# A decoder block on one core: the first modulation row on TensorE, an affine on ScalarE, and lambda computed first

## Chip, core and metric

One NeuronCore of a Trainium2 chip runs the whole kernel. The metric is the device time of one execution in microseconds (us); the median of three runs stands for the kernel. TensorE multiplies matrices, VectorE and GpSimd work elementwise, ScalarE evaluates activations and copies, and SyncE's queue issues most of the DMAs.

## What is computed

The reference is a transformer block on 512 tokens of 1024 channels. What the change touches is the modulation at its start, and lambda, which is used in the differential attention:

```python
cond = jax.nn.silu(c)
mod = cond @ ada_w[l] + ada_b[l]                 # 1024 -> 6 * 1024
sh1, sc1, gt1, sh2, sc2, gt2 = jnp.split(mod[:, None, :], 6, axis=-1)
h = rmsnorm(x, norm1_w[l]) * (1.0 + sc1) + sh1
qa, ka, va, qm, km, vm, om, ip, fp, ga, gm = split_cols(h @ w_in[l], IN_SIZES)
...
lam = (jnp.exp(jnp.sum(lam_q1[l] * lam_k1[l]))
       - jnp.exp(jnp.sum(lam_q2[l] * lam_k2[l])) + lam_init)
y_a = diff_attention(qa, ka, va, lam, subln_w[l], lam_init)
```

After that come the mLSTM branch, the merge, an output projection, a second modulated norm and a PEER expert layer (128 keys, dense for three token tiles, gathered for one).

## The kernel before

The kernel holds 512 tokens as four tiles of 128 (NT) and 1024 channels as eight tiles of 128 (KD). It is written in a tile framework that plans at compile time: it simulates the program with its own costs, and writes out one fixed order of instructions for each engine and one for each DMA queue. Each queue then runs in that order, and an instruction whose operand is late holds everything behind it on its engine. The lines of the source are therefore not the order of execution: for example the memsets of L427 run in the first microseconds. DMAs from SyncE's queue are issued in the planned order too.

**The start stage** (pool `start`, L229 to L303) prepares `hT`, the normalised and modulated input with channels on partitions, and makes the first projections of it: the mLSTM gates (`psg`, called `gate` in the trace), the first head pair's q and the first head pair's k.

- `xt` (four loads of 512 KB) is squared on ScalarE (L265), scaled by the rms (L268), transposed on TensorE (32 transposes, L272), and copied to `xT` on ScalarE (L273).
- The modulation rows are made on VectorE. `ada_early(half)` loads, for shift (`accs[0]`) and scale (`accs[1]`), eight tiles of `ada_w` of 128x512 (256 KB), and `ada_step` (L215 to L219) adds `w * cond` to an accumulator: 8 steps for each of the four (half, row) pairs, 32 in all. Each accumulator still has 128 partitions; `ada_cols` (L221) sums these and turns four columns of 128 channels onto partitions by fp32 matmuls with a column of ones, which write `adac`; VectorE adds the bias (L225).
- Channels 0 to 511 are half 0, channels 512 to 1023 are half 1. For each half, L289 finishes the scale, ScalarE writes `hT_hi` (L291, rounded to fp32r), VectorE repeats the affine at full precision in place in `xT` (L292), and VectorE or, where k % 3 is 2, GpSimd writes `hT_lo = xT - hT_hi` (L293).
- Then the matmuls of this half: `mm3` makes each product out of three fp32r matmuls (hi*hi, hi*lo, lo*hi). Half 0 has 12 of the gate and 48 each of q and k, half 1 the same.
- The weights are split the same way: `load_w` takes raw pieces of 512 KB from two `raw` buffers; ScalarE casts `hi`; VectorE (L181) or GpSimd (L138) subtracts to make `lo`. For k the first piece's `lo` is GpSimd's and the second one's is VectorE's.

**Lambda** (L312 to L324) is computed behind this stage: two products and two sums on one partition of VectorE, an Exp on ScalarE (with its table load), two small VectorE operations, a scaling of `subw`, a matmul that spreads the value to 128 partitions (`psl`), and a copy to `neglam`.

**What follows.** The mix stage handles four head pairs with attention, mLSTM and gates, up to about 640 us. In it `ada_late` (L372) streams the other modulation rows, in 64 loads with two buffers, between the weight pieces on SyncE's queue. The expert layer follows to the end, with TensorE busy 96% of it.

Of the kernel before, what the change touches and what calls it, by code (L numbers as in the profile page):

```python
# [10 lines left out]
F32 = mybir.dt.float32  # L11
# [5 lines left out]
AF = mybir.ActivationFunctionType  # L17
OP = mybir.AluOpType
AX = mybir.AxisListType
PSUM = bass.MemoryType.PSUM  # L20

P = 128
S = 512
D = 1024
KD = D // P
# [5 lines left out]
LAM_INIT = 0.8 - 0.6 * math.exp(-0.3 * 0)  # L31
# [30 lines left out]
def block_kernel(ctx: ExitStack, tc: tile.TileContext, a, out, dbg=None):  # L62
    nc = tc.nc
    dbg = dbg or {}
    V, A, G, T = nc.vector, nc.scalar, nc.gpsimd, nc.tensor
# [13 lines left out]
    def ftile(shape, dt=F32, name=None):  # L79
        return fconst.tile(shape, dt, name=name)  # L80
# [12 lines left out]
    ones = ftile([P, P], F32, "ones")  # L93
# [10 lines left out]
    def load_const(name, shape, src):  # L104
        t = ftile(shape, F32, name)
        nc.sync.dma_start(t, src)
        return t

    cT = load_const("cT", [P, KD], a["cT"])
    cond = ftile([P, KD], F32, "cond")  # L110
# [5 lines left out]
    def rstd(dst, ssq, n, width):  # L116

        V.tensor_scalar(dst, ssq, 1.0 / n, EPS, op0=OP.mult, op1=OP.add)
        G.tensor_tensor(dst, dst, nhalf[:, 0:width], op=OP.pow)
# [15 lines left out]
    def split(hi, lo, src, eng=V):  # L135

        A.copy(hi, src)  # L137
        eng.tensor_tensor(lo, src, hi.bitcast(F32), op=OP.subtract)  # L138
# [5 lines left out]
    def acc_tile(name):  # L144
        return ps_acc.tile([P, 512], F32, tag="acc", name=name)

    def tr_tile(name):
        return ps_tr.tile([P, 512], F32, tag="tr", name=name)


    sh1 = ftile([P, KD], F32, "sh1")
    sc1 = ftile([P, KD], F32, "sc1")
    neglam = ftile([P, 1], F32, "neglam")
# [32 lines left out]
    def mm3(ps, l_hi, l_lo, r_hi, r_lo, start, stop):  # L186
        T.matmul(ps, l_hi, r_hi, start=start, stop=False)  # L187
        T.matmul(ps, l_hi, r_lo, start=False, stop=False)
        T.matmul(ps, l_lo, r_hi, start=False, stop=stop)
# [25 lines left out]
    def ada_step(acc, w, k):  # L215
        if k == 0:
            V.tensor_scalar(acc, w, cond[:, 0:1], None, op0=OP.mult)
        else:
            V.scalar_tensor_tensor(acc, w, cond[:, k:k + 1], acc, op0=OP.mult, op1=OP.add)  # L219

    def ada_cols(acc, n, b0, dst):  # L221
        ps = tr_tile(f"adac_{b0}")
        for k in range(n):
            T.matmul(ps[:, k:k + 1], acc[:, k * P:(k + 1) * P], ones[:, 0:1], start=True, stop=True)
        V.tensor_tensor(dst, ps[:, 0:n], adabT[:, b0:b0 + n], op=OP.add)  # L225


    psg = ps_sc.tile([P, 2, S], F32, tag="sc", name="gate")[:, 0]
    with tc.tile_pool(name="start", bufs=1, side="right") as sp:  # L229
        xts = []  # L230
        for t in range(NT):
            xt = sp.tile([P, D], F32, name=f"xt{t}")
            nc.sync.dma_start(xt, a["x"][t * P:(t + 1) * P, :])
            xts.append(xt)
        adabT = load_const("adabT", [P, 48], a["adabT"])
        n1w = load_const("n1w", [P, KD], a["n1T"])
        accs = [sp.tile([P, D], F32, name=f"ada_acc{i}") for i in range(2)]

        def ada_early(half):
            hs = slice(half * 512, (half + 1) * 512)  # L240
            for i in range(2):
                for k in range(KD):
                    w = sp.tile([P, 512], F32, tag="ada_w", bufs=24, name="ada_w")
                    nc.sync.dma_start(w, a["ada_w"][k * P:(k + 1) * P, i * D + half * 512:i * D + (half + 1) * 512])
                    ada_step(accs[i][:, hs], w, k)
        ada_early(0)
        graw = sp.tile([P, KD, 16], F32, name="graw")
        nc.sync.dma_start(graw, a["w_gate"])
        w_q, w_k = [load_w(w_in, PIECES.index((o,)), n) for o, n in ((O_QA, "q0"), (O_KA, "k0"))]
        ada_early(1)  # L250
        n2w = load_const("n2w", [P, KD], a["n2T"])
        ib = load_const("ib", [8, 1], a["ib"])
        fb = load_const("fb", [8, 1], a["fb"])
        cos_t = load_const("cos_t", [P, NT, 8], a["cos"])
        sin_t = load_const("sin_t", [P, NT, 8], a["sin"])
        lamv = load_const("lamv", [1, 4, 64], a["lamv"])
        convw = load_const("convw", [P, KD, 4], a["convw"])
        convb = load_const("convb", [P, KD], a["convb"])
        subw = load_const("subw", [P, P], a["subln_w"].partition_broadcast(P))
        ssq1 = sp.tile([P, NT], F32, name="ssq1")  # L260
        rs1 = sp.tile([P, NT], F32, name="rs1")
        junk = sp.tile([P, D], BF16, name="junk")
        xT = sp.tile([P, KD, S], F32, name="xT")
        for t in range(NT):
            A.activation(junk, xts[t], AF.Square, accum_out=ssq1[:, t:t + 1])  # L265
        rstd(rs1, ssq1, D, NT)
        for t in range(NT):
            A.activation(xts[t], xts[t], AF.Copy, scale=rs1[:, t:t + 1])  # L268
        for k in range(KD):
            ps = tr_tile("xTp")  # L270
            for t in range(NT):
                T.transpose(ps[:, t * P:(t + 1) * P], xts[t][:, k * P:(k + 1) * P], ident)  # L272
            A.copy(xT[:, k], ps)  # L273


        g_hi, g_lo = [sp.tile([P, KD, P], F32R, name=n) for n in ("g_hi", "g_lo")]
        G.memset(g_hi.bitcast(F32), 0.0)
        G.memset(g_lo.bitcast(F32), 0.0)
        for j in range(2):
            split(g_hi[:, :, j * 32:j * 32 + 8], g_lo[:, :, j * 32:j * 32 + 8], graw[:, :, j * 8:j * 8 + 8])  # L280

        ps_q = [acc_tile(f"q0_{t2}").rearrange("p (t c) -> p t c", t=2) for t2 in range(2)]
        ps_k = ps_sc.tile([P, 2, S], F32, tag="sc", name="k0").rearrange("p b (t c) -> p b t c", t=2)
        ps_k = [ps_k[:, 0], ps_k[:, 1]]
        for half in range(2):
            ks, ks4 = range(4 * half, 4 * half + 4), slice(4 * half, 4 * half + 4)
            ada_cols(accs[0][:, half * 512:], 4, 4 * half, sh1[:, ks4])
            ada_cols(accs[1][:, half * 512:], 4, 8 + 4 * half, sc1[:, ks4])
            V.scalar_tensor_tensor(sc1[:, ks4], sc1[:, ks4], 1.0, n1w[:, ks4], op0=OP.add, op1=OP.mult)  # L289
            for k in ks:  # L290
                A.activation(hT_hi[:, k], xT[:, k], AF.Identity, scale=sc1[:, k:k + 1], bias=sh1[:, k:k + 1])  # L291
                V.tensor_scalar(xT[:, k], xT[:, k], sc1[:, k:k + 1], sh1[:, k:k + 1], op0=OP.mult, op1=OP.add)  # L292
                (G if k % 3 == 2 else V).tensor_tensor(hT_lo[:, k], xT[:, k], hT_hi[:, k].bitcast(F32),  # L293
                                                       op=OP.subtract)
            for k in ks:
                mm3(psg, g_hi[:, k], g_lo[:, k], hT_hi[:, k], hT_lo[:, k], k == 0, k == KD - 1)
            for pss, (whi, wlo) in ((ps_q, w_q), (ps_k, w_k)):
                for t in range(NT):
                    ts_ = slice(t * P, (t + 1) * P)
                    for k in ks:  # L300

                        mm3(pss[t // 2][:, t % 2], hT_hi[:, k, ts_], hT_lo[:, k, ts_], whi[k], wlo[k],
                            k == 0 and t % 2 == 0, k == KD - 1 and t % 2 == 1)  # L303
# [3 lines left out]
    mrg = mrgp.tile([P, NT, D], F32, name="mrg")  # L307
    lx = ExitStack()
    lp = lx.enter_context(tc.tile_pool(name="mix", bufs=1))


    lq = ftile([1, 2, 64], F32, "lp")  # L312
    V.tensor_tensor(lq, lamv[:, 0::2, :], lamv[:, 1::2, :], op=OP.mult)
    ls = ftile([1, 2], F32, "ls")
    V.tensor_reduce(ls, lq, axis=AX.X, op=OP.add)
    le = ftile([1, 2], F32, "le")
    A.activation(le, ls, AF.Exp)
    nl = ftile([1, 1], F32, "nl")
    V.tensor_tensor(nl, le[:, 1:2], le[:, 0:1], op=OP.subtract)
    V.tensor_scalar(nl, nl, LAM_INIT, None, op0=OP.subtract)  # L320
    V.tensor_scalar(subw, subw, 1.0 - LAM_INIT, None, op0=OP.mult)
    psl = tr_tile("psl")
    T.matmul(psl[:, 0:1], ones[0:1, :], nl, start=True, stop=True)
    V.tensor_copy(neglam, psl[:, 0:1])  # L324

    Gr, lf = [lp.tile([P, NT, 256], F32, tag=t_, bufs=1, name=n).rearrange("p t c -> p (t c)")[0:8, 0:S]
              for n, t_ in (("Gr", "g0"), ("lf", "g1"))]
# [341 lines left out]
    for hp in range(4):  # L669
# [26 lines left out]
        for t in range(NT):  # L696
            for u in range(2):
                us = slice(u * P, (u + 1) * P)
                V.scalar_tensor_tensor(ga[:, t, us], y_a[:, t, us], rs[:, 0, t, u:u + 1], ga[:, t, us],  # L699
                                       op0=OP.mult, op1=OP.mult)  # L700
                V.scalar_tensor_tensor(gm[:, t, us], y_m[:, t, us], rs[:, 1, t, u:u + 1], gm[:, t, us],
                                       op0=OP.mult, op1=OP.mult)
# [181 lines left out]
    for k4 in range(2):  # L884
# [3 lines left out]
        ps = tr_tile("hrow")  # L888
# [115 lines left out]
    for n1 in range(KEYS):  # L1004
# [11 lines left out]
        if n1 % (NR // WS) == 0:  # L1016
            i, m0 = n1 % NR // (NR // WS), n1 - n1 % NR
# [18 lines left out]
        for d in range(len(DBS)):  # L1036
            tsl = slice(d * P, (d + 1) * P)
            for m, ahi, alo, vhi, vlo in vparts:
                for i, (l, r) in enumerate(((ahi, vhi), (ahi, vlo), (alo, vhi))):
                    for j in range(2):  # L1040
                        T.matmul(ys[d][j], l[:, tsl], r[:, j * 512:(j + 1) * 512],  # L1041
                                 start=(m == 0 and i == 0), stop=(m == KEYS - 1 and i == 2))
# [86 lines left out]
```

## Time and profile before

| | |
|---|---|
| median of 3 runs | 1923.77 us (1918.71 to 1924.81) |
| the profiled execution | 1921.88 us, its span 1920.1 us |
| TensorE / VectorE / ScalarE / GpSimd busy | 1815.4 / 1431.1 / 813.1 / 686.5 us |
| mean granted TensorE clock | 0.979 |

The span is what the profiler sees between the first and the last instruction; 1.8 us lie around it. A busy share is an average over all stages; what an edit in the first 70 us is worth is read from those 70 us. TensorE's clock has two levels, 1.2 GHz (granted 0.50) and 2.4 GHz (granted 1.00).

### The profile page before, as it was taken

Reading aid. Unit: us, or ns where it says so; the run is one execution under the profiler, and the core shown is the slowest. Engines: PE = TensorE matmul, PEld = TensorE weight load, DVE = VectorE, ACT = ScalarE, POOL = GpSimd, SP = SyncE. Lnnn points to the kernel's source line nnn. Section 1 sums busy time; section 2 is a strip of 40 time slices with the busy share of each in tenths; the row PEclk is TensorE's granted clock in tenths of the full one; section 3 lists DMA queues with packets and bytes.
Section 4 is the critical chain, followed back from the end, with each engine's and each line's share of the span. In section 5 each row is a group of like instructions: output and inputs, shape, how many; then the busy total and the mean of one; then the engine's idle time right before and its main releaser. Section 6 shows DMA issues by size and latency. Waiting matters only on the chain.

```text
span 1920.1 us, 28920 instructions
## 1 busy us (share of the span) xinstructions
PE 1815.4 (95%) x10751; PEld 1631.7 (85%) x10751; DVE 1431.1 (75%) x2748; ACT 813.1 (42%) x1359; POOL 686.5 (36%) x608
## 2 busy tenths in 40 slices
PE   5999899899998998999789999999999999999997
PEld 4989899798986878899678888899888888889896
DVE  7664746646556799999988888887777677767777
ACT  5565464463552423455534433333333332333333
POOL 2523325234235311042300565565333333333433
PEclk8999999999999999999899999999999999999999
DMA  8422415324222232366795899999887887887983
GB/s 281 133 69 84 136 60 158 108 66 144 77 88 91 80 105 88 110 214 243 270 282 177 316 369 340 336 333 340 293 282 282 306 284 277 285 306 255 332 291 132
DMA packets 160283, 404.26 MB, mean 211 GB/s; under 512 B 14471, under 2 KB 63368, under 8 KB 160142
## 3 DMA queue, kind: packets, MB, share of 16 engines
q1 hardware_dynamic: 117026, 240.91, 38.4%
q0 software_dynamic: 36864, 134.23, 19.0%
q10 hardware_dynamic: 6252, 27.28, 3.6%
q8 instruction: 84, 1.38, 0.3%
q14 instruction: 57, 0.47, 0.1%
HBM read 373.52 MB, written 28.84 MB: 210 GB/s over the span
## 4 chain that ended last, share of the span: by engine, by line
PE 61%; DVE 18%; DMA 7%; ACT 6%; issue 4%; POOL 3%; SPq 0%; DVEq 0%; POOLq 0%; ACTq 0%
PE y L1041 22%; PE act L997 7%; PE act L995 7%; PE act L996 7%; DMA gath<-V,idx 3%; DMA ada_w<-ada_w 3%; DVE lo_U L987 1%; DVE ada_acc L219 1%; POOL gath L920 1%; DVE ga L699 1%; DVE lo_V L138 1%; ACT p L489 1%; ACT hi_U L986 1%; PE pr_wq L187 1%; PE wps L872 1%
## 5 line engine op out<-in xcount | busy, mean ns | idle before, releaser
L997 PE MATMUL act<-h_hi,lo_U 128*128 128x384 f32 x1024 | 346.6, 339 | 5.7 <-DVE lo_U L987 5.5
L995 PE MATMUL act<-h_hi,hi_U 128*128 128x384 f32 x1024 | 345.7, 338 | 6.4 <-ACT ga L999 5.4
L996 PE MATMUL act<-h_lo,hi_U 128*128 128x384 f32 x1024 | 344.8, 337 | 0.0
L989 POOL COPY pace<-lo_U 128x1 f32<-128x1 f32 x128 | 103.3, 809 | 570.5 <-DVE lo_U L987 570.3
L1041 PE MATMUL y<-lo_V,ahi 128*128 128x512 f32 x762 | 241.4, 397 | 4.6 <-DVE lo_V L138 4.6
L137 ACT CAST hi_V<-raw_V 128x1024 fp32r<-128x1024 f32 x128 | 134.1, 1050 | 262.4 <-PE y L1041 215.7
L936 DVE SCALAR_TENSOR_TENSOR yg<-gath,act,yg 128x1024 f32<-128x1024 f32 x127 | 162.8, 1282 | 100.1 <-DMA gath<-V,idx 99.0
L1041 PE MATMUL y<-hi_V,alo 128*128 128x512 f32 x762 | 234.6, 394 | 0.0
L1041 PE MATMUL y<-hi_V,ahi 128*128 128x512 f32 x762 | 223.0, 397 | 4.6 <-ACT ahi L137 3.5
L920 POOL DMA_INDIRECT gath<-U,idx x128 | 173.7, 1357 | 118.5 <-DVE junk L926 92.7
L995 PEld LDWEIGHTS act<-h_hi,hi_U 128*128 128x128 f32 x1024 | 193.0, 188 | 12.9 <-ACT ga L999 6.7
L997 PEld LDWEIGHTS act<-h_hi,lo_U 128*128 128x128 f32 x1024 | 192.7, 188 | 12.9 <-DVE lo_U L987 8.9
L996 PEld LDWEIGHTS act<-h_lo,hi_U 128*128 128x128 f32 x1024 | 192.7, 188 | 3.9
L986 ACT CAST hi_U<-raw_U 128x1024 fp32r<-128x1024 f32 x128 | 134.2, 1048 | 125.3 <-PE act L996 96.4
L138 DVE TENSOR_TENSOR lo_V<-raw_V,hi_V 128x1024 fp32r<-128x1024 f32 x128 | 156.0, 1220 | 29.6 <-ACT hi_V L137 29.5
L1041 PEld LDWEIGHTS y<-lo_V,ahi 128*128 128x128 f32 x762 | 142.6, 188 | 37.6 <-DVE lo_V L138 6.5
L987 DVE TENSOR_TENSOR lo_U<-raw_U,hi_U 128x1024 fp32r<-128x1024 f32 x128 | 155.9, 1219 | 22.7 <-ACT hi_U L986 21.2
L137 ACT CAST ahi<-ga 128x384 fp32r<-128x384 f32 x127 | 65.0, 512 | 254.5 <-DVE ga L1026 143.2
L1041 PEld LDWEIGHTS y<-hi_V,alo 128*128 128x128 f32 x762 | 142.6, 187 | 34.1 <-DVE alo L138 0.2
L1041 PEld LDWEIGHTS y<-hi_V,ahi 128*128 128x128 f32 x762 | 142.2, 189 | 31.9 <-ACT ahi L137 3.7
L926 DVE SCALAR_TENSOR_TENSOR junk<-gath,hrow 128x1024 bf16<-128x1024 f32 x128 | 156.1, 1220 | 14.7 <-DMA gath<-U,idx 13.7
L920 POOL DMA_INDIRECT gath<-V,idx x128 | 150.2, 1173 | 38.7 <-issue 30.3
(462 smaller groups left out, 4128.6 us busy)
## 6 DMA issues: line engine op xcount, KB each, us to landing
raw_U<-UT SPq DMA_DIRECT2D x128, 512.0 KB, 5.3
raw_V<-V SPq DMA_DIRECT2D x128, 512.0 KB, 5.8
ada_w<-ada_w SPq DMA_DIRECT2D x96, 256.0 KB, 3.8
W_dram<-st ACTq DMA_DIRECT2D x24, 960.0 KB, 4.7
W<-W_dram SPq DMA_DIRECT2D x60, 384.0 KB, 9.0
raw_wq<-wq SPq DMA_DIRECT2D x16, 512.0 KB, 3.5
raw_q<-w_in SPq DMA_DIRECT2D x8, 512.0 KB, 4.4
raw_k<-w_in SPq DMA_DIRECT2D x8, 512.0 KB, 3.6
```

The lines of the kernel that those rows point to most:

```text
L137: A.copy(hi, src)
L138: eng.tensor_tensor(lo, src, hi.bitcast(F32), op=OP.subtract)
L920: G.indirect_dma_start(out=t_, out_offset=None, in_=src, in_offset=bass.IndirectOffsetOnAxis(ap=idx0[:, s:s + 1], axis=0))
L926: V.scalar_tensor_tensor(junk2, u, 1.0, hrow, op0=OP.mult, op1=OP.mult, accum_out=act[:, s:s + 1])
L936: V.scalar_tensor_tensor(yg, v, act[:, s:s + 1], yg, op0=OP.mult, op1=OP.add)
L986: A.copy(hi, raw)
L987: V.tensor_tensor(lo, raw, hi.bitcast(F32), op=OP.subtract)
L989: with tc.issue_after(G.tensor_copy(pace, lo[:, 0:1].bitcast(F32)).ins):
L995: T.matmul(ps, hi[:, ks], h_hi[:, k], start=(k == 0), stop=False)
L996: T.matmul(ps, hi[:, ks], h_lo[:, k], start=False, stop=False)
L997: T.matmul(ps, lo[:, ks], h_hi[:, k], start=False, stop=(k == KD - 1))
L1041: T.matmul(ys[d][j], l[:, tsl], r[:, j * 512:(j + 1) * 512], start=(m == 0 and i == 0), stop=(m == KEYS - 1 and i == 2))
```

## The change

Three things. (1) In half 0, the shift's row is no longer accumulated on VectorE: eight fp32 matmuls with one column of `cond` as weights and a 128x512 tile of `ada_w` as the moving operand accumulate one row of 512 in PSUM, ScalarE copies it to partition 0 of `accs[0]`, and `ada_cols` turns it with matmuls over one partition. (2) In half 0, the full precision affine of `xT` is made on ScalarE, right behind `hT_hi` of the same k. (3) Lambda and its load are put ahead of the start stage; the scaling of `subw` is put behind its load.

```diff
-    def ada_cols(acc, n, b0, dst):
+    def ada_cols(acc, n, b0, dst, rows=P):
         ps = tr_tile(f"adac_{b0}")
         for k in range(n):
-            T.matmul(ps[:, k:k + 1], acc[:, k * P:(k + 1) * P], ones[:, 0:1], start=True, stop=True)
+            T.matmul(ps[:, k:k + 1], acc[0:rows, k * P:(k + 1) * P], ones[0:rows, 0:1], start=True, stop=True)
         V.tensor_tensor(dst, ps[:, 0:n], adabT[:, b0:b0 + n], op=OP.add)
+    lamv = load_const("lamv", [1, 4, 64], a["lamv"])
+    lq = ftile([1, 2, 64], F32, "lp")
+    V.tensor_tensor(lq, lamv[:, 0::2, :], lamv[:, 1::2, :], op=OP.mult)
...
+    psl = tr_tile("psl")
+    T.matmul(psl[:, 0:1], ones[0:1, :], nl, start=True, stop=True)
+    V.tensor_copy(neglam, psl[:, 0:1])
@@ ada_early
             for i in range(2):
+                on_pe = half == 0 and i == 0
+                ps = acc_tile("ada_row")[0:1] if on_pe else None
                 for k in range(KD):
                     w = sp.tile([P, 512], F32, tag="ada_w", bufs=24, name="ada_w")
                     nc.sync.dma_start(w, a["ada_w"][k * P:(k + 1) * P, i * D + half * 512:i * D + (half + 1) * 512])
-                    ada_step(accs[i][:, hs], w, k)
+                    if on_pe:
+                        T.matmul(ps, cond[:, k:k + 1], w, start=(k == 0), stop=(k == KD - 1))
+                    else:
+                        ada_step(accs[i][:, hs], w, k)
+                if on_pe:
+                    A.copy(accs[i][0:1, hs], ps)
@@ constants
-        lamv = load_const("lamv", [1, 4, 64], a["lamv"])
         subw = load_const("subw", [P, P], a["subln_w"].partition_broadcast(P))
+        V.tensor_scalar(subw, subw, 1.0 - LAM_INIT, None, op0=OP.mult)
@@ for half in range(2)
-            ada_cols(accs[0][:, half * 512:], 4, 4 * half, sh1[:, ks4])
+            ada_cols(accs[0][:, half * 512:], 4, 4 * half, sh1[:, ks4], P if half else 1)
...
-                V.tensor_scalar(xT[:, k], xT[:, k], sc1[:, k:k + 1], sh1[:, k:k + 1], op0=OP.mult, op1=OP.add)
+                if half == 0:
+                    A.activation(xT[:, k], xT[:, k], AF.Identity, scale=sc1[:, k:k + 1], bias=sh1[:, k:k + 1])
+                else:
+                    V.tensor_scalar(xT[:, k], xT[:, k], sc1[:, k:k + 1], sh1[:, k:k + 1], op0=OP.mult, op1=OP.add)
@@ behind the start stage
-    lq = ftile([1, 2, 64], F32, "lp")
...
-    V.tensor_copy(neglam, psl[:, 0:1])
```

## Rows read from the trace of the kernel before

**Rows 1.** The page: span and instructions.

```profile
span 1920.1 us, 28920 instructions
```

**Rows 2.** Busy time by stretch: length, engines in turn, clock, DMA share, GB/s.

```profile
26.00:46.00 20.00, 13.31 (x76) 11.85 (x76) 19.93 (x30) 6.41 (x8) 5.52 (x3) 0.76 0.65 215
46.00:70.00 24.00, 24.00 (x176) 23.33 (x177) 12.97 (x19) 13.81 (x19) 12.91 (x21) 0.93 0.43 127
...
90.00:100.00 10.00, 8.52 (x48) 6.71 (x47) 5.00 (x12) 7.80 (x15) 2.35 (x1) 1.00 0.10 33
...
70.00:640.00 570.00, 534.74 (x3809) 493.09 (x3807) 332.90 (x616) 297.05 (x600) 204.60 (x138) 0.97 0.31 99
```

**Rows 3.** The same view in stretches of 2 us.

```profile
26.00:28.00 2.00, 0.00 (x0) 0.00 (x0) 2.00 (x3) 0.14 (x1) 1.41 (x1) 0.50 1.05 386
...
48.00:50.00 2.00, 2.00 (x14) 2.00 (x13) 1.97 (x5) 2.00 (x4) 0.31 (x1) 0.68 0.51 201
```

**Rows 4.** Timeline of VectorE: start, duration, instruction, [idle before <-releaser].

```profile
10.59 5.47 DVE L219 SCALAR_TENSOR_TENSOR ada_acc<-ada_w,cond,ada_acc 128x512 f32<-128x512 f32 x7
...
25.20 2.49 DVE L217 TENSOR_SCALAR ada_acc<-ada_w,cond 128x512 f32<-128x512 f32 x1
...
29.18 0.54 DVE L292 TENSOR_SCALAR xT<-xT,sc,sh 128x512 f32<-128x512 f32 x1
...
32.48 1.50 DVE L292 TENSOR_SCALAR xT<-xT,sc,sh 128x512 f32<-128x512 f32 x1
...
39.48 0.27 DVE L313 TENSOR_TENSOR lp<-lamv 1x128 f32<-1x128 f32 x1
39.68 2.88 DVE L219 SCALAR_TENSOR_TENSOR ada_acc<-ada_w,cond,ada_acc 128x512 f32<-128x512 f32 x1
...
44.36 0.75 DVE L219 SCALAR_TENSOR_TENSOR ada_acc<-ada_w,cond,ada_acc 128x512 f32<-128x512 f32 x1
45.03 0.13 DVE L320 TENSOR_SCALAR nl<-nl 1x1 f32<-1x1 f32 x1
```

**Rows 5.** Timeline of ScalarE.

```profile
27.86 2.93 ACT L291 ACTIVATE hT_hi<-xT,sh,sc 128x512 fp32r<-128x512 f32 x4 [2.96 <-DVE sc L289]
38.49 1.05 ACT L137 CAST hi_k<-raw_k 128x1024 fp32r<-128x1024 f32 x1 [7.70 <-DMA raw_k<-w_in]
...
42.89 1.03 ACT L178 CAST hi_k<-raw_k 128x1024 fp32r<-128x1024 f32 x1
```

**Rows 6.** Timeline of GpSimd.

```profile
24.98 2.43 POOL L138 TENSOR_TENSOR lo_q<-raw_q,hi_q 128x1024 fp32r<-128x1024 f32 x1 [13.39 <-ACT hi_q L137]
...
39.62 2.39 POOL L138 TENSOR_TENSOR lo_k<-raw_k,hi_k 128x1024 fp32r<-128x1024 f32 x1 [5.92 <-ACT hi_k L137]
```

**Rows 7.** Timeline of TensorE's matmuls.

```profile
17.10 5.29 PE L272 MATMUL xTp<-ident,xt 128*128 128x128 f32 x24 [0.46 <-ACT xT L273]
...
41.46 0.28 PE L189 MATMUL q<-hi_q,hT_lo 128*128 128x256 f32 x1
...
45.26 0.47 PE L224 MATMUL adac<-ones,ada_acc 128*128 128x1 f32 x3 [2.61 <-DVE nl L320]
...
46.39 0.56 PE L188 MATMUL k<-lo_k,hT_hi 128*128 128x256 f32 x1
...
67.72 0.38 PE L323 MATMUL psl<-nl,ones 1*128 1x1 f32 x2
68.03 0.39 PE L187 MATMUL pt_v<-hi_v,hT_hi 128*128 128x256 f32 x1
```

**Rows 8.** Issues of SyncE's DMA queue.

```profile
34.83 0.38 SPq L173 DMA_DIRECT2D raw_k<-w_in  x1
```

**Rows 9.** Line 395 on TensorE, four fp32 matmuls: ns min/median/max.

```profile
L395 PE MATMUL adar<-ada_acc,ones x8: 590/592/697, 326.9 to 485.7; 128*128 128x512 f32 x8
```

**Rows 10.** The chain that ended last, 0 to 140 us: start, us, what.

```profile
77.07 4.44 DMA ada_w<-ada_w
...
82.26 3.43 DVE lo_vm L181
```

More of the change, by code (lines that the diff above doesn't have):

```diff
@@ L219, in ada_step @@
             V.scalar_tensor_tensor(acc, w, cond[:, k:k + 1], acc, op0=OP.mult, op1=OP.add)
-    def ada_cols(acc, n, b0, dst):
+    def ada_cols(acc, n, b0, dst, rows=P):
         ps = tr_tile(f"adac_{b0}")
         for k in range(n):
-            T.matmul(ps[:, k:k + 1], acc[:, k * P:(k + 1) * P], ones[:, 0:1], start=True, stop=True)
+            T.matmul(ps[:, k:k + 1], acc[0:rows, k * P:(k + 1) * P], ones[0:rows, 0:1], start=True, stop=True)
         V.tensor_tensor(dst, ps[:, 0:n], adabT[:, b0:b0 + n], op=OP.add)
+    lamv = load_const("lamv", [1, 4, 64], a["lamv"])
+    lq = ftile([1, 2, 64], F32, "lp")
+    V.tensor_tensor(lq, lamv[:, 0::2, :], lamv[:, 1::2, :], op=OP.mult)
+    ls = ftile([1, 2], F32, "ls")
+    V.tensor_reduce(ls, lq, axis=AX.X, op=OP.add)
+    le = ftile([1, 2], F32, "le")
+    A.activation(le, ls, AF.Exp)
+    nl = ftile([1, 1], F32, "nl")
+    V.tensor_tensor(nl, le[:, 1:2], le[:, 0:1], op=OP.subtract)
+    V.tensor_scalar(nl, nl, LAM_INIT, None, op0=OP.subtract)
+    psl = tr_tile("psl")
+    T.matmul(psl[:, 0:1], ones[0:1, :], nl, start=True, stop=True)
+    V.tensor_copy(neglam, psl[:, 0:1])
     psg = ps_sc.tile([P, 2, S], F32, tag="sc", name="gate")[:, 0]
@@ L309, in block_kernel @@
     lp = lx.enter_context(tc.tile_pool(name="mix", bufs=1))
-    lq = ftile([1, 2, 64], F32, "lp")
[L313 to L323, printed above, removed]
-    V.tensor_copy(neglam, psl[:, 0:1])
     Gr, lf = [lp.tile([P, NT, 256], F32, tag=t_, bufs=1, name=n).rearrange("p t c -> p (t c)")[0:8, 0:S]
```

## Prediction

> **What bounds the kernel now.** I read the page first, for the span [rows 1], then the busy time by stretches [rows 2], because the change lies in the first 70 us and only the waits there can move. From 26 to 46 us TensorE works 13.31 of 20 us, and VectorE works 19.93 of 20: in this stretch VectorE sets the pace. Behind it, from 70 to 640 us, TensorE works 534.74 of 570 us, so there TensorE sets it, and what the start saves moves everything behind it forward. The expert stage that follows contains nothing of the change.
>
> Then I read the timelines. On TensorE, half 0 of q ends at 41.74 us (41.46 + 0.28). It is followed by the columns of half 1's modulation (adac), the last of which start only at 45.26 us after an idle time of 2.61 us, and only behind these, at 46.39 us, does k of half 0 go on [rows 7]. The idle time is put down to the last lambda step, but the matmul reads the accumulators: VectorE's last step L219 on them runs from 44.36 to 45.11 us, 0.15 us before [rows 4]. From 46 to 70 us TensorE is busy all 24.00 us [rows 2], so a microsecond taken off this wait is a microsecond off the end of k.
>
> What else must be there for k? Its raw weights are issued at 34.83 us [rows 8] and cast at 38.49 us [rows 5]; GpSimd writes the low part of the first piece from 39.62 to 42.01 us [rows 6]. So k of half 0 could go on at 42.0 us, 4.4 us before it does. This is the room that the change has here, and the next thing that is late.
>
> **The change, part by part.**
>
> *VectorE, half 0.* Eight of the 32 accumulator steps go: one at about 0.5 us and seven in 5.47 us [rows 4], 6 us in all, before 23 us. But VectorE's next work, the steps of half 1, needs loads that come behind the weights of q, and GpSimd's subtraction for q starts only at 24.98 us, right behind their cast [rows 6]. I count this gain as nothing; the arrival of the data hides it. The bounds are 0 and 1 us.
>
> *VectorE, the affine.* Four instructions L292 of half 0 leave it, the first 0.54 us, the last of the four 1.50 us [rows 4]; with two more like the first this is 3.1 us out of the stretch that sets the end.
>
> *VectorE, lambda.* Five instructions between 39.48 us (0.27 us) and 45.03 us (0.13 us) [rows 4]; the scaling of subw stays in the start stage, the four others go to its front, where VectorE waits for its first load anyway (its steps begin near 10 us). With about 0.2 us each that is 0.8 us.
>
> So the last step would end at 45.11 - 3.1 - 0.8 = 41.2 us. One step of these 16 took 2.88 instead of 0.75 us, from 39.68 us, beside GpSimd's subtraction for k that ran from 39.62 to 42.01 us [rows 4, 6]. Without this stall the sum is 39.1 us, that is, the steps would be through before that subtraction begins. Both bounds lie below or near 42.0 us. The first step of half 1 shows the same thing: 2.49 us beside GpSimd's subtraction for q [rows 4, 6].
>
> The Trainium skill (Advanced Engine Details and Errata, VectorE Performance Modes) says that GpSimd and those VectorE instructions that use the second port block each other, and gives two-port modes to operations with a single tensor source. The affine L292 is of that kind and its 1.50 us agrees; the stalled L219 of 2.88 us has two tensor sources, and there the row decides. By the rule alone the last step would end at 39.1 us; by the row up to 41.2 us.
>
> *TensorE, k.* Adac's last columns take 1.1 us from their start to k (45.26 to 46.39 us) [rows 7]. With VectorE at 39.1 to 41.2 us they end at 40.3 to 42.5 us; the low weights are there at 42.0 us. I take 42.3 us for the point that is now at 46.39 us: **-4.1 us**, with bounds of -2 and -4.4 us.
>
> *TensorE, the row.* The eight new matmuls have 512 fp32 columns. The nearest row is L395, of the same shape, which appears as two records of 0.59 us each [rows 9], so at most 8 x 1.18 = 9.4 us, and about two thirds of that if the two records overlap. They can begin when the first loads land, near 10 us; TensorE has eight transposes to do before 17.1 us and 24 in 5.29 us then [rows 7]. At 0.22 us each, 1.8 of the 7.1 us up to 17.1 us are taken, and 5.3 us are free. Between 1 and 4 us of the row run over into the transposes, and hT_hi, which starts at 27.86 us [rows 5], may start up to 2.6 us earlier (the shift is done, and the stalled step need not stand in front of it) or up to 2 us later. I take no change. What hides it: half 0 of q must only be through by 42 us, and it ends at 41.7 us already with the old affine.
>
> *ScalarE.* It gets the four affines, at 0.73 us each by hT_hi (2.93 us for four) [rows 5], so hT_lo of the last k waits for 5.9 us of ScalarE instead of 2.9 us. In the old order the last affine on VectorE ended at 34.0 us [rows 4], 6.1 us behind the start of hT_hi; with pairs on ScalarE it ends 5.9 us behind. The pace of half 0 is the same or slightly better: 0 us. Copying the row costs one ScalarE instruction among the copies of xT. This adds a wait: VectorE's hT_lo now waits for ScalarE, and the steps of half 1 are queued behind it, then adac, then k.
>
> The Trainium skill (ScalarE: Activation LUTs, Rules for kernel authors) advises VectorE, not ScalarE, for additions and multiplications. The rows agree on the price, 0.73 against 0.54 us; by the rule the four would cost 0.8 us more, but on an engine that works 6.41 of these 20 us. That VectorE is the engine that is full is what the rule leaves open.
>
> *Lambda's other parts.* The matmul leaves TensorE's queue between 67.72 and 68.03 us [rows 7]: **-0.3 us**. Its table load and Exp leave ScalarE; they lay between the two casts of k, 38.49 and 42.89 us [rows 5]. The load goes from behind to ahead of the x loads on SyncE's queue; one issue costs about 0.4 us (0.38 in [rows 8]), which delays all loads behind it, and takes one issue away in front of the raw k. I take 0 us, with bounds of -0.4 and +0.4 us.
>
> *The clock.* With no matmul from 26 to 28 us the granted clock was 0.50, the lower level; behind the 2.6 us wait it was still down to 0.68 on the mean at 48 to 50 us, where it came back [rows 3]. At half speed each us of it does half a us of work, so the low stretch from about 46 to 49 us costs now some 1.1 to 1.5 us. If half 0 of q ends earlier, the wait in front of 42 us is as long as before, or longer, and the low stretch too. I take **+0.3 us**, bounds -1.1 us (no wait, the clock stays up) and +1.7 us (twice the low stretch of now, and a little).
>
> Sum: -4.1 - 0.3 + 0.3 = -4.1 us. On the profiled execution, span 1920.1 us [rows 1] and 1.8 us around it, 1921.9 us, this gives 1917.8 us. The median of the runs, 1923.8 us, is 1.9 us above that execution; on it the forecast is **1919.7 us**, 0.2% below.
>
> **The rivals.**
>
> *A. The gain grows downstream: 1916 us or less.* With lambda out of ScalarE the second cast of k is up to 3.4 us earlier (42.89 less the end of the first, 39.54) [rows 5], and with it the buffer for the next raw weights. TensorE idles 1.5 us between 90 and 100 us and 35 us from 70 to 640 us [rows 2], where the low weights of vm stand on the chain with 3.43 us [rows 10]. If weights that come earlier fill the 1.5 us and another 2 us of the sort, the gain is 4.1 + 3.5 = 7.6 us: 1916.2 us. For it: these waits begin with casts and loads of this stage. Against it: TensorE is full from 46 to 70 us [rows 2], so most of the earlier weights wait anyway.
>
> *B. ScalarE becomes late for VectorE: 1922 us.* If hT_hi starts 2 us late because the row's matmuls ran over, hT_lo holds back the steps of half 1. It decides once VectorE's last step slips past 40.9 us, when adac and no longer the weights is last. A slip of 3 us puts it at 42.1 to 44.2 us, k at 43.3 to 45.3 us, and leaves 1 to 3 us of gain: about 1922 us.
>
> *C. Slower by more than 0.3%: 1933 us.* The planner writes new orders from new due times for everything behind. SyncE's queue mixes weight pieces with the other modulation's loads, which wait for a buffer; one such load stands on the chain with 4.44 us [rows 10]. If the new order puts a load that must wait ahead of a weight piece that TensorE needs, three times over the four head pairs, that is 13.3 us lost against 4.1 gained: 1933 us. It turns slower by 0.3% from 9.9 us lost. For it: the order is fixed and the chain holds these loads; against it: the same loads and buffers as before, and nearly the same shift for all that follows.
>
> **How the numbers follow.** 0.3%, 5.8 us here, is what a measurement of this kernel can tell from no change. The forecast has 0.50, A 0.30, B 0.10, C 0.10. The forecast's own range is -0.2 to -6.2 us by the bounds above, so a small part of it (0.06) crosses the bound to faster, and A nearly all. Faster: 0.36. Same: most of the forecast, B, and little of A: 0.55. Slower: C without its lower part, 0.09. The range of 8 in 10 takes the forecast, B and two thirds of A: from 1913 us (A with 7 us filled downstream, 4.1 + 7 = 11 us less) to 1926 us (nothing gained, 2 us lost to the new order).
>
> **What would show it.** Right: VectorE's last step of half 1 ends at 39 to 41.5 us; k's second matmul of half 0 starts near 42 us, right behind GpSimd's subtraction; no affine of half 0 and no lambda on VectorE after 23 us; the last k matmul ends near 63.5 us instead of 67.8 us. Wrong: the 24 transposes end more than 2 us behind 22.4 us, or hT_hi starts after 30 us (the row is dearer than I took it); hT_lo waits for ScalarE with half 1's steps behind it (B); or the start is 4 us shorter and the 640 us mark is not (C, or a gain lost in the mix stage).

## The result and the profile after

The changed kernel takes 1947.72 us (median of 4 runs, 1945.22 to 1950.05), the kernel before 1924.29 us beside it (4 runs): ratio 1.0109, 95% interval 1.0086 to 1.0132. By the ratio it is 21 us slower (23.4 us by these two medians), where 4 us less was forecast. The page's span answers to [rows 1]; 28 us more for 24 instructions more (this execution lies 2.3 us above its median, that of before 2.4 us below).

```profile
span 1948.2 us, 28944 instructions
```

**The start.** TensorE's timeline, which answers to [rows 7]:

```profile
10.37 5.70 PE L264 MATMUL ada_row<-ada_w,cond 128*1 128x512 f32 x8 [4.66 <-DMA ada_w<-ada_w]
16.00 0.44 PE L295 MATMUL xTp<-ident,xt 128*128 128x128 f32 x2
...
25.28 1.14 PE L295 MATMUL xTp<-ident,xt 128*128 128x128 f32 x8 [0.78 <-ACT xT L296]
...
33.42 0.77 PE L187 MATMUL gate<-hT_hi,g_hi 128*128 128x512 f32 x1 [3.46 <-ACT hT_hi L314]
...
52.78 0.28 PE L189 MATMUL k<-hi_k,hT_lo 128*128 128x256 f32 x1
52.90 0.95 PE L225 MATMUL adac<-ones,ada_acc 128*128 128x1 f32 x8
55.26 0.53 PE L187 MATMUL gate<-hT_hi,g_hi 128*128 128x512 f32 x1 [1.41 <-ACT hT_hi L314]
...
58.00 0.79 PE L188 MATMUL gate<-hT_lo,g_hi 128*128 128x512 f32 x1 [0.93 <-DVE hT_lo L319]
...
73.29 0.28 PE L189 MATMUL k<-hi_k,hT_lo 128*128 128x256 f32 x1
```

Two things are to be seen. The row's first eight records stand in front of the first transposes, so these start at 16.00 us (12.82 us before) and the last eight at 25.28 us. And adac, the last columns of half 1, now stands behind all of k of half 0, at 52.90 us (45.26 us in [rows 7]). Only then can half 1 begin; TensorE waits 1.41 and 0.93 us. ScalarE, which answers to [rows 5]:

```profile
20.92 0.58 ACT L268 COPY ada_acc<-ada_row 1x512 f32<-1x512 f32 x1 [4.62 <-PE ada_row L264]
21.40 1.05 ACT L296 COPY xT<-xTp 128x512 f32<-128x512 f32 x2
...
32.46 2.93 ACT L314 ACTIVATE hT_hi<-xT,sh,sc 128x512 fp32r<-128x512 f32 x4 [4.83 <-DVE sc L312]
35.30 2.91 ACT L316 ACTIVATE xT<-xT,sh,sc 128x512 f32<-128x512 f32 x4
...
54.39 2.93 ACT L314 ACTIVATE hT_hi<-xT,sh,sc 128x512 fp32r<-128x512 f32 x4
```

hT_hi of half 0 starts 4.60 us later than in [rows 5], that of half 1 at 54.39 us (47.02 us before). In the source each affine stands right behind its hT_hi; the planned order has the four hT_hi first and the four affines behind them, from 35.30 us. VectorE, which answers to [rows 4]:

```profile
25.91 0.48 DVE L217 TENSOR_SCALAR ada_acc<-ada_w,cond 128x512 f32<-128x512 f32 x1
26.43 4.29 DVE L219 SCALAR_TENSOR_TENSOR ada_acc<-ada_w,cond,ada_acc 128x512 f32<-128x512 f32 x3
...
38.23 1.76 DVE L219 SCALAR_TENSOR_TENSOR ada_acc<-ada_w,cond,ada_acc 128x512 f32<-128x512 f32 x1
...
40.66 3.54 DVE L219 SCALAR_TENSOR_TENSOR ada_acc<-ada_w,cond,ada_acc 128x512 f32<-128x512 f32 x2
...
53.89 0.16 DVE L226 TENSOR_TENSOR sc<-adac,adabT 128x4 f32<-128x4 f32 x1 [4.14 <-PE adac L225]
```

VectorE is through with its last step at 44.2 us (45.11 us before), although it began half 1's steps later, at 25.91 us (25.20 us before). What it hands over then lies for 8.7 us until TensorE comes to adac. The clock follows the two waits; the busy time by stretches, columns as in [rows 2]:

```profile
46.00:56.00 10.00, 8.59 (x70) 8.46 (x70) 2.31 (x4) 3.61 (x5) 1.44 (x1) 0.98 0.39 131
56.00:62.00 6.00, 5.07 (x20) 4.39 (x19) 5.44 (x7) 1.32 (x2) 2.45 (x2) 0.50 0.28 90
```

From 56 to 62 us the granted clock is 0.50, the lower level. The last k matmul starts at 73.29 us, 5.8 us later than before.

**The mix stage** adds next to nothing. The planned orders of all engines and of SyncE's queue from about 100 to 960 us are the same as before, and the distance between the two traces (how much later the changed kernel reaches the same instruction) is 5.5 us at 521 us and 6.2 us at 739 us.

**The expert stage** costs the rest: 7 us of distance at 960 us, 17 us at 1,410 us, 28 us at the last matmul of the layer (1907.7 and 1936.1 us). No line of the change is there, but the planner wrote another order. In this stage U and V are the experts' weights: each raw tile of 512 KB is cast to a high part on ScalarE and subtracted to a low part on VectorE, and single rows of U and V are gathered by GpSimd's DMAs. W holds the gates of the dense tiles, `s` the scores of the gathered one. The new order shows first on SyncE's queue, kernel before:

```profile
965.89 2.96 SPq L1020 DMA_DIRECT2D W<-W_dram  x3
968.90 0.81 SPq L965 DMA_DIRECT2D s<-s_dram  x1
...
1060.17 3.58 SPq L1020 DMA_DIRECT2D W<-W_dram  x4
```

and after:

```profile
975.87 0.97 SPq L1031 DMA_DIRECT2D W<-W_dram  x2
976.89 0.54 SPq L976 DMA_DIRECT2D s<-s_dram  x1
...
1077.14 5.33 SPq L1031 DMA_DIRECT2D W<-W_dram  x4
1082.57 6.34 SPq L1024 DMA_DIRECT2D raw_V<-V  x2
```

One piece of W that stood ahead of the load of `s` now stands behind it, and from there everything is arranged differently. At 1,077 us four pieces of W (384 KB each), the first eight gathers of rows of U and the raw V loads meet. GpSimd's issues, first and last of the eight:

```profile
1077.37 1.20 POOL L931 DMA_INDIRECT gath<-U,idx  x1 [0.18 <-issue]
...
1090.78 1.68 POOL L931 DMA_INDIRECT gath<-U,idx  x1 [0.60 <-DVE junk L937]
```

The kernel before issues four pieces at 1060.17 us too, but three gathers go with them, the third at 1067.00 us, and the next only at 1076.83 us; TensorE waits 1.03 us:

```profile
1067.00 2.11 POOL L920 DMA_INDIRECT gath<-U,idx  x1 [1.66 <-DVE gate L828]
1076.83 1.17 POOL L920 DMA_INDIRECT gath<-U,idx  x1 [7.72 <-DVE room L821]
```

```profile
1073.72 1.42 PE L1041 MATMUL y<-hi_V,ahi 128*128 128x512 f32 x5 [1.03 <-ACT hi_V L137]
```

In the changed kernel ScalarE waits longer for raw V, and TensorE for ScalarE:

```profile
1098.93 1.04 ACT L137 CAST hi_V<-raw_V 128x1024 fp32r<-128x1024 f32 x1 [10.11 <-DMA raw_V<-V]
```

```profile
1100.02 2.50 PE L1052 MATMUL y<-hi_V,ahi 128*128 128x512 f32 x5 [5.49 <-ACT hi_V L137]
```

Further on VectorE loses the time. Two of its additions of gathered rows wait for their DMAs, and the low half of the next U tile is queued behind them:

```profile
1555.34 1.28 DVE L947 SCALAR_TENSOR_TENSOR yg<-gath,act,yg 128x1024 f32<-128x1024 f32 x1 [1.52 <-DMA gath<-V,idx]
1559.83 1.28 DVE L947 SCALAR_TENSOR_TENSOR yg<-gath,act,yg 128x1024 f32<-128x1024 f32 x1 [3.20 <-DMA gath<-V,idx]
1561.03 1.22 DVE L138 TENSOR_TENSOR lo_V<-raw_V,hi_V 128x1024 fp32r<-128x1024 f32 x1
1562.16 1.22 DVE L998 TENSOR_TENSOR lo_U<-raw_U,hi_U 128x1024 fp32r<-128x1024 f32 x1
```

The cast that lo_U needs had ended at 1556.6 us; TensorE waits 3.63 us for lo_U. That VectorE takes its instructions strictly in turn is also what the Trainium skill says (Perfetto Trace Analysis, Tensor Engine Instruction, in a note on the other engines); the rows agree. Grouped, from 1,000 us to the end, first before, then after (busy, mean ns, idle time before them and what ended it):

```profile
L997 PE MATMUL act<-h_hi,lo_U 128*128 128x384 f32 x736 | 247.6, 337 | 3.2 <-DVE lo_U L987 3.0
...
L1041 PE MATMUL y<-hi_V,ahi 128*128 128x512 f32 x726 | 211.5, 395 | 1.0 <-ACT hi_V L137 1.0
```

```profile
L1008 PE MATMUL act<-h_hi,lo_U 128*128 128x384 f32 x738 | 249.7, 338 | 10.9 <-DVE lo_U L998 10.9
...
L1052 PE MATMUL y<-hi_V,ahi 128*128 128x512 f32 x732 | 214.0, 397 | 7.4 <-ACT hi_V L137 5.5 <-ACT ahi L137 2.0
```

These two groups alone wait 14.1 us more, of the 21 us by which the distance grows behind 960 us; the waits for lo_V and alo add 2.5 us, and the rest I did not locate.

### The profile page after: what moved, and what is told of

Same layout as the page of the kernel before. It is cut to its first block, busy times and chain, and to the rows that moved or that the text cites. A ratio compares the mean times of both kernels' runs of the same rounds, so it can differ in the third digit from the quotient of the medians.

```text
span 1948.2 us, 28944 instructions
## 1 busy us (share of the span) xinstructions
PE 1833.8 (94%) x10767; PEld 1640.5 (84%) x10767; DVE 1426.5 (73%) x2736; ACT 814.5 (42%) x1364; POOL 697.1 (36%) x608
## 4 chain that ended last, share of the span: by engine, by line
PE 56%; DVE 17%; DMA 9%; issue 5%; ACT 5%; POOL 4%; DVEq 0%; SPq 0%; POOLq 0%; ACTq 0%
PE y L1052 20%; PE act L1008 7%; PE act L1006 6%; PE act L1007 6%; DMA gath<-V,idx 4%; DMA ada_w<-ada_w 3%; DVE lo_U L998 2%; POOL gath L931 1%; DVE ada_acc L219 1%; DVE ga L710 1%; DMA raw_V<-V 1%; PE wps L883 1%; PE wps L882 1%; DVE gm L712 1%; PE pr_wq L187 1%
## 5 line engine op out<-in xcount | busy, mean ns | idle before, releaser
L1000 POOL COPY pace<-lo_U 128x1 f32<-128x1 f32 x128 | 113.1, 886 | 575.7 <-DVE lo_U L998 575.0
```

The costliest lines, as they stand in the source:

```text
L1000: with tc.issue_after(G.tensor_copy(pace, lo[:, 0:1].bitcast(F32)).ins):
```

## The experiments

My theory after the result: two losses, some 6 us in the start and the rest from another planned order of the expert stage (in short, the expert order). The rivals: a part of the change costs by itself wherever it stands, or a late start lengthens the expert stage.

### The three parts alone (e1, e2, e3)

Each is the kernel before with one part of the change's diff: e1 with lambda and its load ahead of the start, e2 with the row on TensorE and its copy on ScalarE, e3 with the affine:

```diff
+                if half == 0:
+                    A.activation(xT[:, k], xT[:, k], AF.Identity, scale=sc1[:, k:k + 1], bias=sh1[:, k:k + 1])
+                else:
+                    V.tensor_scalar(xT[:, k], xT[:, k], sc1[:, k:k + 1], sh1[:, k:k + 1], op0=OP.mult, op1=OP.add)
```

> Lambda first and nothing else; the planned order from 100 us to the end is that of the kernel before. Theory (the loss is two losses: some 6 us in the start stage, made by the row on TensorE, and some 22 us in the expert stage, made by another planned order): no loss, 1921 to 1926 us, with the 24 transposes ending near 22.4 us as before. Rival (each part of the change costs by itself, the expert stage merely passes it on): some of the 23 us, 1928 us or more.

> Only the shift's row of half 0 on TensorE; the planned order of the mix and expert stages is that of the kernel before. Theory: the start is longer by 4 to 7 us, the copies of xT begin near 21 us, the last k matmul of the start is near 73 us; the expert stage adds less than 3 us: 1928 to 1932 us. Rival (a later start is what makes the expert stage longer, by collisions of its transfers): the expert stage adds 10 us or more, 1938 us or more.

> Only the affine of half 0 on ScalarE; the planned order of the mix stage is that of before, the one of the expert stage differs from it, and is close to that of the changed kernel. Theory: the start changes by 3 us at most, and the expert stage takes 10 to 24 us more: 1932 to 1948 us. Rival (the affine is harmless, the loss comes from the row and what follows from it): 1919 to 1926 us.

Measured against the kernel before on the same chip (1927.25 us): e1 1.0009 (0.9984 to 1.0034), e2 1.0017 (0.9998 to 1.0035), e3 1.0079 (1.0046 to 1.0112). In e2 the last k matmul starts at 72.7 us, 5.1 us late, and the whole is 3.7 us longer by the medians, no more than the start is late (the interval reaches from 0 to 6.7 us): a late start does not make the expert stage 18 us longer. In e3 it starts at 66.2 us, 1.3 us early, and the whole loses 15 us, all of it behind 960 us (the distance is 0.8 us there). e3 has another expert order; e1 and e2 have that of the kernel before, instruction for instruction on every engine of this stage. TensorE's wait for raw V in e3, as in the changed kernel:

```profile
1095.35 2.93 PE L1044 MATMUL y<-hi_V,ahi 128*128 128x512 f32 x6 [7.49 <-ACT hi_V L137]
```

### The order alone (e4)

The kernel before, all its work unchanged, with one ordering edge: the third group's pieces of W are issued behind the second group's, as in the changed kernel.

```diff
+                with tc.issue_after(w_loads[WS - 1]) if NR <= n1 < 2 * NR else ExitStack():
+                    w_loads.append(nc.sync.dma_start(Wnext[:, bs], W_dram[...]).ins)
```

> The kernel before with all its work unchanged; only the planner is told to issue the four loads of W for the third group of eight keys behind those for the second, an edge of order on one queue without a wait. With it the planned order of SyncE's and GpSimd's queues in the expert stage becomes that of the run with the affine alone. Theory: the same times as before up to 960 us, and 10 to 24 us more behind it: 1934 to 1948 us. Rival (the order of the expert stage is of no weight): 1920 to 1927 us.

Measured: 1947.64 us, 1.0107 (1.0072 to 1.0142), as slow as the changed kernel. Its orders of SyncE and GpSimd behind 960 us are those of e3, and those of the changed kernel but for two issues. The same groups as above, from 1,000 us on:

```profile
L997 PE MATMUL act<-h_hi,lo_U 128*128 128x384 f32 x736 | 250.8, 341 | 14.3 <-DVE lo_U L987 14.3
...
L1044 PE MATMUL y<-hi_V,ahi 128*128 128x512 f32 x732 | 213.9, 397 | 6.1 <-ACT hi_V L137 6.1
```

So an order without any change of work makes these waits. Whether the affine costs something beside it is left to e7.

### One expert order for all (e5, e6, e7)

If each piece of W is issued behind the raw V load of its own key, the planner writes the same expert order for the kernel before (e5), for the whole change (e6) and for the affine alone (e7).

```diff
-        nc.sync.dma_start(vraw, a["V"][n1 * P:(n1 + 1) * P, :])
+        vload = nc.sync.dma_start(vraw, a["V"][n1 * P:(n1 + 1) * P, :]).ins
...
-                nc.sync.dma_start(Wnext[:, bs], W_dram[...])
+                with tc.issue_after(vload):
+                    nc.sync.dma_start(Wnext[:, bs], W_dram[...])
```

> The kernel before, with one ordering edge per piece: each load of a piece of W (384 KB) in the expert stage is issued behind the raw V load of its own key, instead of four pieces in a row. Theory 1 (the planned order of the expert stage is what costs; in the slower orders four pieces of W, eight gathers and the raw V loads meet near 1,070 us and ScalarE waits for raw V): the wait of TensorE for hi_V near 1,070 to 1,100 us stays under 3 us, and the time is 1,915 to 1,935 us. Theory 2 (the burst has nothing to do with that wait): it is 5 us or more, as in the changed kernel (5.49 us), and the time is about 1,945 us. The start stage is untouched: k ends at 67 to 69 us.

> The changed kernel with the same edges, so that its expert stage has the planned order of e5, instruction for instruction. Theory 1 (the order carries all that the start does not): slower than e5 by 4 to 7 us, the delay of the start alone (+5.8 us at the end of k), and the offset between the two traces stays there to the end. Rival (the parts of the change cost something downstream in any order, as a late start that the expert stage multiplies): slower than e5 by 15 to 25 us.

> The kernel before with the affine of half 0 on ScalarE alone, and the edges of e5, again with the expert order of e5. Theory 1: e5 less 1 us (its start is 1.3 us shorter in e3), so the 20 us that the affine alone lost in e3 are gone. Rival (the affine on ScalarE costs by itself): e5 plus 15 to 25 us.

Measured, against 1928.15 us: e5 1931.32 us, 1.0020 (1.0002 to 1.0037); e6 1933.88 us, 1.0025 (1.0007 to 1.0042); e7 1931.37 us, 1.0017 (0.9997 to 1.0038). Under one order the whole change costs 2.6 us over e5, somewhat less than I had expected, and the affine nothing: the 15 us of e3 are gone. With the pieces spread the wait for raw V is small (e5):

```profile
1086.70 1.66 PE L1042 MATMUL y<-hi_V,ahi 128*128 128x512 f32 x6 [0.76 <-ACT hi_V L137]
```

But the waits for lo_U remain in e5 (10.5 us from 1,000 us on), so this order is no better than that of before. And the edges moved the gathers too (the first of U at 1052.4 us, 1060.9 us before): whether the pieces or the gathers make the crowd at 1,077 us was not tried apart.

### The copy of the row on VectorE (e8)

```diff
-                    A.copy(accs[i][0:1, hs], ps)
+                    V.tensor_copy(accs[i][0:1, hs], ps)
```

> The whole change, only the copy of the row out of PSUM moved from ScalarE to VectorE. Its expert stage has the planned order of the kernel before. Theory 1: the copies of xT no longer stand behind the row (they start near 16.5 us instead of 21.4 us), hT_hi of half 0 starts 1 to 4 us earlier than in the changed kernel (32.46 us), k ends 2 to 6 us behind the kernel before, and the whole time is 2 to 7 us above it, 1,925 to 1,933 us. If the row's matmuls among the transposes are the cause and not the copy, the copies still start near 21 us and k ends 5 to 6 us late. Rival (the change costs downstream in any order): 1,945 us.

Measured: 1931.01 us, 1.0014 (0.9995 to 1.0033): the whole change in the expert order of before costs 2.9 us by the medians and, going by the ratios, 18 us less than the changed kernel does. In the start I had blamed the copy, since ScalarE waits 4.62 us for the row with the copies of xT behind it. The row of e8 says otherwise:

```profile
20.29 1.08 ACT L297 COPY xT<-xTp 128x512 f32<-128x512 f32 x2 [4.30 <-PE xTp L296]
```

Without the row's copy on its engine ScalarE waits 4.30 us for the transposes. hT_hi of half 0 comes 1.9 us earlier than in the changed kernel (30.59 us), the last k matmul starts 0.8 us earlier (72.5 us). The copy is a small part; the row's matmuls among the transposes, which end at 25.3 us (26.4 us with the copy, 22.4 us before the change), are the larger one.

### Half 1's columns ahead of k (e9, e10)

```diff
             for pss, (whi, wlo) in ((ps_q, w_q), (ps_k, w_k)):
+                if half == 0 and pss is ps_k:
+                    cols(1)
```

`cols(half)` holds the two `ada_cols` of that half and the line that finishes the scale, which stood at the head of the loop. e9 is e6 with this edit, e10 is e8 with it.

> The kernel of e6 (whole change, spread loads of W, expert order of e5) with the last columns of half 1's modulation written ahead of k of half 0, so that TensorE's order has them at its place 97 instead of 145, 48 matmuls earlier. Theory 1 (the delay of the start comes mostly from these columns standing behind k of half 0, where TensorE then waits 1.4 and 0.9 us and runs at half clock): the columns start at 47 to 48 us instead of 52.9, hT_hi of half 1 at 48 to 49.5 us instead of 54.4, no wait of TensorE over 0.9 us and no granted clock of 0.50 between 53 and 62 us, k ends at 68 to 69.5 us instead of 73.3, and the time is 2 to 5 us under e6. Theory 2 (the row among the transposes delays everything by 5 us, whatever the order behind it): k still ends at 72 us or later and the time is that of e6.

> The kernel of e8 (whole change, copy of the row on VectorE, expert order of the kernel before) with the columns of half 1 ahead of k of half 0. Theory 1: k ends at 66 to 69 us (72.5 in e8), and the time is that of the kernel before within 3 us, ratio 0.998 to 1.0015; the change with both its losses taken away gives nothing back, because half 0 still starts some 3 us later. Theory 2: as e8, ratio 1.0014 or more.

Measured, against 1927.99 us: e9 1927.60 us, 1.0001 (0.9987 to 1.0016), 6.3 us under e6 by the medians (4.6 us by the ratios); e10 1924.88 us, 0.9976 (0.9960 to 0.9991), 6.1 us under e8 (7.3 us). Each keeps the expert order of its pair, so this is the start alone. TensorE in e10:

```profile
35.33 0.80 PE L188 MATMUL gate<-hT_lo,g_hi 128*128 128x512 f32 x1 [0.65 <-DVE hT_lo L324]
45.47 0.95 PE L224 MATMUL adac<-ones,ada_acc 128*128 128x1 f32 x8
```

Between 35.33 us and the last k matmul (66.3 us) no row of it has a wait. In e9 the clock stays up, where the changed kernel has 0.50 from 56 to 62 us:

```profile
54.00:62.00 8.00, 8.00 (x61) 7.64 (x60) 1.47 (x3) 4.80 (x8) 5.79 (x13) 1.00 0.47 150
```

The last k matmul starts at 67.2 us in e9 and 66.3 us in e10, against 73.3 and 72.5 us: even earlier than I had expected, though half 0 still starts 2.6 us (e10) to 3.9 us (e9) late. The row makes half 0 late, but that reaches the end of k only in the order with the columns behind k.

### Two of the four affines (e11)

The kernel before with lambda first and the affines of k = 2 and 3 of half 0 on ScalarE, no row on TensorE.

```diff
+                if half == 0 and k >= 2:
```

> The kernel before with lambda first and with two of the four affines of half 0 (k = 2 and 3) on ScalarE; no row on TensorE; its expert stage has the planned order of the kernel before. Theory 1: half of what e3 and e1 save in the start (k ends 0.5 to 2 us earlier, at 65.5 to 67 us), nothing is lost behind it, ratio 0.998 to 1.0005: no measurable difference, and not the 1.0079 of e3. Rival (an affine on ScalarE costs by itself): about 1.004, half of e3's loss.

Measured: 1924.48 us, 0.9981 (0.9964 to 0.9999), the expert order of before, the last k matmul at 67.0 us. With the order kept an affine on ScalarE costs nothing. e10 and e11 are 0.2% below the kernel before. Their starts, in single traces, are 1.3 and 0.5 us shorter, of the 3.1 and 3.5 us; the rest I did not locate. The interval of e11 leaves room for its not being there, that of e10 reaches to 1.7 us.

## Why the prediction was wrong

**The step that failed: "The expert stage that follows contains nothing of the change."** Its work doesn't change, its order does, and that is 18 to 20 us of the 21: e4 loses 1.07% by the order alone, and the whole change in the old order (e8) loses 0.14%. Rival C had the kind, a new planned order, but in the mix stage, among the ada loads, where nothing was rearranged, at 13 us and a chance of 0.10. What decides is not how much an edit moves: one edge turned the order (e4), four affines turned it (e3), two with lambda did not (e11), the row did not (e2), and the whole change, four affines included, did not once the row's copy stood on VectorE (e8). Why the planner turns in one case and not in the other, no run shows.

**"Adac's last columns ... from their start to k."** The -4.1 us rested on adac keeping its place ahead of k, and on VectorE. The planner put these columns behind all 48 matmuls of k of half 0 (one stood ahead of them before). Half 1 waited for it, and TensorE paid 1.41 + 0.93 us of waits and about 2.5 us by the clock (5.07 us busy at half speed). This is only about 1 us more than the old wait of 2.61 us and the low clock behind it had cost: from the first gate matmul to the last of k the kernel before takes 38.7 us, the changed one 39.9 us. But e9 takes 34.4 us and e10 34.8 us. So what the order cost is the room in which the late half 0 would have been made up. With adac in its place (e10) the last k matmul starts at 66.3 us, 1.3 us before the kernel before, not 4.

VectorE gave back less than was computed. Its last 16 steps took from 25.91 to 44.20 us, 18.3 us, where they took 19.9 us before: 1.6 us less, and the forecast was 3.9 us at least. One reason can be read: the affine's stall (1.50 instead of 0.54 us) did not leave with the affine. A step now takes 1.76 us at 38.23 us, beside GpSimd's hT_lo from 37.59 to 39.45 us.

**"hT_hi ... I take no change."** The bound was 2 us late, it was 4.6 us, and it was not hidden: q of half 0 had 0.3 us of room up to 42 us and ended at 47.3 us. At most 9.4 us were allowed for the row, and it runs from 10.37 to 20.9 us. The free time in front of the transposes was 4.3 us rather than 5.3 us, because the first eight take 0.69 us a pair and not 0.44 us, and it could not be used in pieces: the planner put the first four matmuls, eight records of 5.70 us, ahead of the first transpose, and the last transposes ended 4 us later. Both signs named for this came, transposes over 2 us behind 22.4 us and hT_hi after 30 us.

**"Copying the row costs one ScalarE instruction."** It costs a wait of 4.62 us on an engine that takes its work in turn, but of these only about 1 us is its own (e8).

**Rivals A and B.** A fell with the start, which grew instead of shrinking. B had hT_hi late and VectorE's last step at up to 44.2 us, and that is where it ended; but adac did not wait for it, so B's price of a smaller gain was not the one paid.

**Right:** the affine on ScalarE does hardly any harm to half 0 (its last q matmul starts at 41.62 us in e3, 41.46 us before) and saves in the start: the last k matmul starts at 66.2 us in e3 and 64.0 us in e7, at 67.5 to 69.1 us in the three runs with the start of before (that kernel, e4, e5). Lambda first is nothing that can be measured (e1, 1.0009; its k is where it was, 67.5 us). The stall of L219 beside GpSimd came back: two steps in 3.54 us at 40.66 us, where GpSimd's subtraction for k runs from 41.01 to 43.66 us. This instruction has two tensor sources and stalls all the same, which that section of the Trainium skill (Advanced Engine Details and Errata, VectorE Performance Modes) does not give; the rows decide. In e3 it is lambda's first product, also of two tensors, that stands beside this subtraction: 2.48 us instead of 0.27 us. So taking an instruction off VectorE did not take its stall off.

## What to carry to other kernels

Where a planner writes the order, an edit's price has two parts, the work and the new order of everything behind it; compare the two planned orders before the times, and find the first place where they part. To cost an edit by itself, hold the order behind it fixed with an edge that gives both versions the same one. And where work is taken off the engine that sets the pace, look where its consumer stands in the next engine's queue: e10 gained 6 us over e8 by moving four tiny matmuls (eight records) ahead of k.

## What the runs showed that I had not expected

The row's first five records, which start up to 13.7 us, took 1.05 us on the mean and the later ones 0.59 us, the same instruction (ns min/median/max):

```profile
L264 PE MATMUL ada_row<-ada_w,cond x16: 591/592/1057, 10.4 to 20.3; 128*1 128x512 f32 x16
```

They are spaced 0.85 us, then 0.43 us, a factor of two, as between the two clock levels; yet the granted clock reads 1.00 from 8 to 16 us. So the durations speak for the lower level and the granted row does not; that it was the clock is read from this factor alone. The Trainium skill (TensorE: Matmul & The Clock Gate, Seeing it yourself) warns that the clock's trace events can't be fully trusted, which agrees with these rows. It made the row about 2 us dearer than its price at 327 us in [rows 9].

Executions of the same order scatter in the start: the kernel before, e4 and e5 have the same one, and adac's last columns start at 45.1 to 45.3 us in all three, but the last k matmul starts at 67.5, 69.1 and 68.8 us. The granted clock behind the wait for adac differs, in the same stretch of the kernel before, e4 and e5:

```profile
46.00:54.00 8.00, 8.00 (x53) 7.91 (x54) 6.63 (x12) 3.87 (x5) 1.54 (x1) 0.79 0.22 66
```

```profile
46.00:54.00 8.00, 8.00 (x45) 8.00 (x46) 6.39 (x12) 3.86 (x5) 1.53 (x1) 0.61 0.23 66
```

```profile
46.00:54.00 8.00, 8.00 (x47) 8.00 (x47) 6.22 (x12) 3.87 (x5) 1.52 (x1) 0.65 0.29 92
```

So a difference of under 2 us between the starts of two single traces is within this scatter.

They scatter in the mix stage too: the kernel before, e4 and e5 have one order until well behind 760 us, and reach the expert layer's first activation at 747.1, 749.8 and 752.6 us. A distance of some 5 us between two single traces behind the start says little by itself.
